# Weight loads and accumulating transfers put on their queues by the planner's due times, in a hybrid attention and recurrence block

## The chip, the cores and the metric

The kernel runs on one core of one Trainium2 chip. The metric is the time of one execution on the device, in microseconds (us); lower is better. The core has a matrix engine (TensorE, PE in the profile, with its weight loads as a row of their own, PEld), VectorE (DVE), ScalarE (ACT), GpSimd (POOL) and SyncE (SP). Each engine works through its own instructions in the order in which the program was written out. Transfers (DMAs) are issued by SP, POOL and ACT; an instruction that issues one waits on its engine's queue until what it needs is there, and what stands behind it on that engine waits with it.

## The reference, cut to what matters

One layer of a residual block on 512 tokens (and 16 learned meta tokens ahead of them) of width 2048. All of it is float32.

```python
h = rms_norm(x, norm_g)
proj = h @ w_in                       # 2048 x 12368
(q_a, k_a, v_a, z_a, q_i, k_i, w_i, q_b, f_b, i_b, z_b, gates) = split(proj)
# branch A: an indexer scores keys, the top 128 are kept per query, attention over them
# branch B: gated linear recurrence in chunks of 64
y = stack([attention * silu(z_a), rms_norm(recurrence) * silu(z_b)])
p = einsum('btnc,ncd->btnd', y, w_branch)      # 2 x 1024 x 2048
merged = sum(sigmoid(gates) * p, axis=2)
return x + merged @ w_out                      # 2048 x 2048
```

## The kernel before, in words

**Products.** A float32 product is made of three TensorE products of rounded parts: every operand is split into a high part (a ScalarE copy that rounds, `wh`) and the remainder (a VectorE subtraction, `wl`). This is done for every weight tile on the way: `hi_lo` (line 417). The three tags of `wh` and of `wl` are used in turn (`NWS = 3`), so the preparation of one operand has to wait for the product that used the tag three operands ago.

**Pairs.** Most of `w_in`, and all of `w_out`, is worked through in *pairs*: a 2x2 block of weights, for which a seven-product scheme (Strassen's, in Winograd's form) takes the place of eight products. There are 44 pairs of `w_in` and 8 of `w_out`. A pair loads four weight chunks of 512 KB, named "11", "21", "22", "12" in this order (line 378), and makes four sums from them:

- the first sum, `s1 = 21 + 22`, and the second, `s2 = s1 + 11`, are VectorE additions into tiles of their own (`sum` in the profile);
- the third, `s3`, is "21" with "11" added in place by an accumulating transfer that POOL issues (`E.dma_add`, line 122, in the profile L123 POOL `raw<-raw`);
- the fourth, `s4`, is "12" with `s2` added in place in the same way (`raw<-sum`).

The seven products run in the order 11, s2, 12, s3, s1, 22, s4 (line 382). Each is 24 matmuls (8 tiles of rows, three parts each), in `run_pair` (line 1549) and, for `w_out`, `run_out` (line 1650). The operand of product i+3 is prepared (`prep_op`, line 487) right after the matmuls of product i are written out, so "12" of a pair is prepared at the end of the pair before.

**What sets the order.** The program is written out by Python code that keeps a clock for each compute engine (`Core`, line 51): every instruction is charged a cost, and starts after what it reads and overwrites. `E.clk["pe"]` is TensorE's clock on this plan, `E.ac[tile]` the time of a tile's last access, `E.wr[tile]` that of its last write. The plan charges an accumulating transfer 4.0 us on POOL and does not cover loads. After every three matmuls `pump` (line 254) lets generator tasks go on (norms, rotary embedding, the recurrence, attention) whose times have come. These tasks write instructions of all engines: on SP the stores and loads that turn k, v and q by way of device memory (`fan`, four DMAs of 64 KB each, line 824; `qay<-qd`, line 874), on POOL other fans, the powers `x ** -0.5` of the norms (line 118) and the gate loads.

**Where the transfers stand.** Before the change a step's transfers are written out right at that step:

```python
def load_upto(i):
    while state["dma"] <= min(i, len(stream) - 1):
        load_chunk(stream[state["dma"]])
        state["dma"] += 1
...
        used = {"s3": 2, "22": 3, "s4": 4}.get(nm)
        if used:
            load_upto(first + used - 1 + NRAW)
```

There are six buffers for weight chunks (`NRAW = 6`). When `s3` has been prepared, the two chunks that go into the buffers of "11" and "21" are queued on SP, when "22" has, the one that goes into its buffer, and when `s4` has, the one into "12"'s. Each waits on SP until the VectorE subtraction, or the accumulating transfer, that uses the buffer last is done. In the seven products, after product 1 the fourth sum of this pair is queued on POOL, and after products 3, 4 and 5 the first, second and third sum of the next pair are made (lines 1587 to 1590, 1705 to 1708).

**Stages.** The nine first jobs are not pairs; their ten low parts (`wl<-raw`) come from accumulating transfers too, which the change does not touch. In the span of the profile the first jobs run until about 145 us, pairs of `w_in` until about 1090 us (k, v and q between 370 and 540 us, then the recurrence), the product with `w_branch` until about 1310 us, and the pairs of `w_out` until the end.

Of the kernel before, what the change touches and what calls it, by code (L numbers as in the profile page):

```python
# [210 lines left out]
def hybrid_kernel(ctx, tc, x, meta, vecs, w_in, rows, w_branch, w_out,  # L211
# [8 lines left out]
    E = Core(nc)  # L220
# [25 lines left out]
    def spawn(gen, prio=1):  # L246
# [4 lines left out]
        tasks.insert(i, t)  # L251
        return t

    def pump(limit=3000.0):
        moved = True
        while moved:
            moved = False
            for t in list(tasks):
                now = E.clk["pe"]
                if t.prio > 5 and hold:  # L260
                    continue
                lim = limit if t.prio < 5 else 1200.0
                if t.t + MARGIN <= now and E.clk["dve"] < now + lim and E.clk["act"] < now + limit:
                    if not t.done and t.step():
                        moved = True
                        break
# [85 lines left out]
    stream = []  # L352
# [31 lines left out]
                preps_.append(op)  # L384
                self.ops.append(op)

    state = {"dma": 0, "split": 0}
    early = []
    NRAW = 6
    NWS = 3  # L390

    def load_chunk(ch):
        j, i = ch["job"], ch["i"]
        r = wp.tile([128, 1024], F32, name=f"raw{i}", tag=f"raw{i % NRAW}")
        nk, k0, c0, nc_ = ch["nk"], ch["k0"], ch["c0"], ch["ncols"]
        src = {"br": w_branch[0, j.n], "out": w_out[0]}.get(j.kind, w_in2)
        v = r[:, :nk * nc_].rearrange("p (k n) -> p k n", k=nk)
        s = src[128 * k0:128 * (k0 + nk), c0:c0 + nc_].rearrange("(k p) n -> p k n", p=128)
        nc.sync.dma_start(v, s)
        ch["raw"] = r  # L400

    def load_upto(i):
        while state["dma"] <= min(i, len(stream) - 1):
            load_chunk(stream[state["dma"]])
            state["dma"] += 1

# [38 lines left out]
    def split_chunk(k, ch):  # L445
        load_upto(ch["i"])
        m = ch["nk"] * ch["ncols"]
        r, nk, n = ch["raw"], ch["nk"], ch["ncols"]
        ch["h"], ch["l"] = [], []
        if k < 4:  # L450
            for g in range(2):
                h, l = slot("eh", F32R), slot("el", F32R)
                w = 4 * n
                E.act(h[:, :w], r[:, w * g:w * g + w], AF.Copy)
                (E.ptt if k > 1 else E.tt)(l[:, :w], r[:, w * g:w * g + w], h[:, :w].bitcast(F32), OP.subtract)
                early.extend((h, l))
                ch["h"] += [h[:, n * i:n * i + n] for i in range(4)]
                ch["l"] += [l[:, n * i:n * i + n] for i in range(4)]
        else:
            j = ch["job"]  # L460
            o = lead(YHOME[j.n], DIST - DBR) if j.kind == "br" else lead((HA, HB)[ch["k0"] // 8], 32)
            h, l = hi_lo(k, r[:, :m], m, o, 0, (n, 24) if j.kind == "br" and j.n == 0 and j.c0 in (0, 1024) else None)
            ch["h"], ch["l"] = cut([h], n), cut(l, n)
        load_upto(ch["i"] + NRAW)

    def sum_1(pr):
        if not hasattr(pr, "s1"):
# [4 lines left out]
    def sum_2(pr):  # L472
        if not hasattr(pr, "s2"):
            pr.s2 = wp.tile([128, 1024], F32, name=f"sum2_{pr.raw['11']['i']}", tag="s2")
            E.tt(pr.s2, pr.s1, pr.raw["11"]["raw"], OP.add)

    def sum_3(pr):
        if not hasattr(pr, "s3"):
            pr.s3 = pr.raw["21"]["raw"]
            E.dma_add(pr.s3, pr.raw["11"]["raw"])  # L480

    def sum_4(pr):
        if not hasattr(pr, "s4"):
            pr.s4 = pr.raw["12"]["raw"]
            E.dma_add(pr.s4, pr.s2)

    def prep_op(k, op):

        pr, nm = op["pair"], op["name"]
        first = pr.raw["11"]["i"]  # L490
        load_upto(first + (0 if nm == "11" else 2 if nm == "s2" else 3))
        raw = {c: ch["raw"] for c, ch in pr.raw.items() if "raw" in ch}
        if nm in raw:
            src = raw[nm]
        else:
            for f in (sum_1, sum_2, sum_3, sum_4)[:int(nm[1]) if nm != "s1" else 1]:
                f(pr)
            src = {"s1": pr.s1, "s2": pr.s2, "s3": raw["21"], "s4": raw["12"]}[nm]
        home, half = HOME[nm]
        if pr.kind == "out":  # L500
            h, l = hi_lo(k, src, 1024, lead(0, MRES[MOP[nm]], True))
        else:
            h, l = hi_lo(k, src, 1024, lead(home, 1056 * half + 4 * (264 - pr.w)), 0 * (nm == "22"))
        w = pr.ncols
        op["h"], op["l"] = cut([h], w), cut(l, w)
        used = {"s3": 2, "22": 3, "s4": 4}.get(nm)
        if used:
            load_upto(first + used - 1 + NRAW)


    cvec = cp.tile([128, 35], F32, name="cvec")
# [1037 lines left out]
    def run_pair(pr, nxt, late, last):  # L1549

        w = pr.w
        bk, W, V = {}, slice(0, w), slice(w, 2 * w)
        for i, (wn, tn, bn, on_) in enumerate(SEVEN):
            op = pr.ops[i]
            split_upto(op["prep"] + 2)
            if not on_:
                bk[bn] = B1.get("p" + bn)
            b = bk[bn][:, W]
            for k in range(8):
                if pr is pairs[0] and i == 1 and k not in placed:  # L1560
                    place_t3(k)
                if pr is pairs[0] and i == 3:
                    place_t4(k)
                th, tl = (t[:, 264 - w:264] for t in (TB[k][tn] if i else (hH[k], hL[k])))
                st_ = k == 0 and not on_
                E.mm(b, op["h"][k], th, st_, False, loose=True)
                E.mm(b, op["h"][k], tl, False, False, loose=True)
                E.mm(b, op["l"][k], th, False, k == 7, loose=True)
                pump(1500.0 if i in (0, 1, 4) and k > 2 else 3000.0)
            if i == 0:  # L1570
                p1 = main_slot("p1")
            elif i == 1:
                E.tt(p1[:, V], p1[:, W], b, OP.subtract)
            elif i == 3:
                E.tt(p1[:, W], b, p1[:, W], OP.subtract)
                B1.put(bk["y"])
            elif i == 4:
                g2 = main_slot("g2")
                E.tt(g2[:, V], p1[:, W], b, OP.subtract)
            elif i == 5:  # L1580
                E.tt(g2[:, W], p1[:, W], b, OP.add)
                B1.put(bk["w"])
            elif i == 6:
                E.tt(g1[:, V], p1[:, V], b, OP.add)
                B1.put(bk["z"])
                S.put(p1)
            if i == 1:
                sum_4(pr)
            if i > 2 and i < 6 and nxt:
                (sum_1, sum_2, sum_3)[i - 3](nxt)  # L1590
            split_upto(op["prep"] + 3)
            if i == 0:
                E.act(p1[:, W], b, AF.Copy)
            if late:
                late.pop(0)()
            if i == 2:
                g1 = main_slot("g1")
                E.act(g1[:, W], b, pr.f)
                B1.put(bk["x"])
            elif i == 5:  # L1600
                late.append(lambda g=g2: pr.done[1](g))
            elif i == 6:
                late.append(lambda g=g1: pr.done[0](g))
            if pr is pairs[-2] and i == 2:
                fetch(0, 0)
            if last:
                if i == 2:
                    fetch(0, 1)
                    first_y.extend(load_y(4, 6, nc.gpsimd))
                elif i == 3:  # L1610
                    S.put(*hH[:8], *hL[:8])
                    for h in range(8):
                        yH[1, h], yL[1, h] = slots("yH", 2, F32R, YHOME[1])
                    while len(y_out) < 8:
                        pump(1e9)
                        if len(y_out) < 8:
                            E.clk["pe"] += 200
                    ysplit = split_y(first_y + [kept[6], kept[7]], 1)
                elif i == 4:
                    S.order = [2, 3, 0, 1]  # L1620
                    S.put(*[t for k in range(8) for t in TB[k]["tiles"][:2]])
                elif i == 5:
                    S.put(*[TB[k]["tiles"][2] for k in range(8)])
                elif i == 6:
                    S.put(*hH[8:], *hL[8:])
                    late.pop(0)()
                    load_gates(1, 0)
                if i in (4, 5):
                    for _ in range(4):
                        next(ysplit, None)  # L1630
# [19 lines left out]
    def run_out(pr, nxt):  # L1650
# [10 lines left out]
        for i, (wn, tn, _, _) in enumerate(SEVEN):  # L1661
# [19 lines left out]
            if r == 1 and not ends:  # L1681
# [20 lines left out]
                else:  # L1702
                    E.tt(q(0, 1), q(0, 1), b, OP.add)
                    store_q(c, 0, 1)
            if i == 1:
                sum_4(pr)
            elif i > 2 and i < 6 and nxt:
                (sum_1, sum_2, sum_3)[i - 3](nxt)
# [390 lines left out]
```

## Time and profile before

| | us |
|---|---|
| median of 3 runs | 1471.97 (1471.61 to 1472.19) |
| the profiled execution | 1472.37 |
| its span in the trace | 1470.6 |
| PE busy / PEld busy | 1446.4 / 1413.1 |
| DVE / ACT / POOL busy | 1188.7 / 715.5 / 270.7 |
| weight loads on SP: 192 of `w_in`, 32 of `w_branch`, 32 of `w_out` | 4.6, 4.9, 4.4 from issue to landing (median) |
| accumulating transfers `raw<-raw` / `raw<-sum`, 52 each | 5.4 / 5.8 from issue to landing (median) |

Matmuls are pipelined, so the busy time of PE holds whatever it is given without a break; only the breaks are idle time. A line of the waits reads: who waited (engine, tile, line) for whom, the sum in us, how often, and the longest. A line of the timeline reads: start, duration, engine, line, operation, tiles as out<-in, shapes, how many in a row, and in brackets the idle time of the engine before it with what ended it. "POOL" and "SPq" lines of a transfer show how long it took to issue, not to land. Tile names carry no numbers: `raw` is any of the six weight chunks.

### The profile page before, as it was taken

To read this page: it belongs to the slowest core of one execution; us is meant where nothing else is said; L and a number is where in the kernel's file an instruction comes from. 1 tells how busy PE (TensorE), PEld (TensorE's weight loads), DVE (VectorE), ACT (ScalarE), POOL (GpSimd) and SP (SyncE) were. 2 spreads that over 40 slices of the span, in tenths; PEclk is the share of its full clock that TensorE was granted. 3 is DMA by queue.
4 is the path that set the end of the run, shared out by engine and by line. 5 is a ranking of instruction groups with operands and counts; after the bars stand their busy time and mean duration, and the time that the engine had idled before them with its cause. 6 is when DMAs were issued, how large, how long until landed. Compare 5 with 4: busy or idle time off the path is not lost.

```text
span 1470.6 us, 33183 instructions
## 1 busy us (share of the span) xinstructions
PE 1446.4 (98%) x13384; PEld 1413.1 (96%) x13384; DVE 1188.7 (81%) x2017; ACT 715.5 (49%) x1172; POOL 270.7 (18%) x344
## 2 busy tenths in 40 slices
PE   7999999999999999999999999999999999999999
PEld 6888999999999999999999999999999999999998
DVE  6789899999988788878787887779676666877776
ACT  5567554544544454444444444444466762434433
POOL 2210000002223320001001010000347410102222
PEclk9999999999999999999999999999999999999999
DMA  9375577788787987678677777858896444558783
GB/s 270 78 166 128 133 175 191 185 200 194 202 207 202 235 205 178 165 173 189 168 192 175 171 182 180 187 135 203 192 279 184 131 121 118 158 137 218 209 222 98
DMA packets 335929, 262.35 MB, mean 178 GB/s; under 512 B 32596, under 2 KB 303520, under 8 KB 335776
## 3 DMA queue, kind: packets, MB, share of 16 engines
q1 hardware_dynamic: 306304, 174.54, 41.6%
q0 software_dynamic: 23968, 79.40, 27.7%
q10 hardware_dynamic: 5504, 6.29, 1.3%
q8 instruction: 105, 1.72, 0.5%
q14 instruction: 48, 0.39, 0.1%
HBM read 170.43 MB, written 29.98 MB: 136 GB/s over the span
## 4 chain that ended last, share of the span: by engine, by line
PE 88%; DMA 4%; DVE 4%; ACT 2%; issue 1%; POOL 1%; SPq 0%; ACTq 0%; DVEq 0%; POOLq 0%
PE px L97 16%; PE pz L97 14%; PE py L97 14%; PE pg L97 12%; PE po L97 9%; PE pw L97 8%; PE pg L99 6%; DMA raw<-sum 2%; PE psc L99 1%; DMA raw<-in_w_in_dram 1%; DVE wl L114 1%; PE phl L99 1%; PE pov L97 1%; ACT wh L107 1%; PE plg L99 1%
## 5 line engine op out<-in xcount | busy, mean ns | idle before, releaser
L107 ACT ACTIVATE wh<-raw 128x1024 fp32r<-128x1024 f32 x306 | 324.1, 1061 | 466.5 <-PE pz L97 110.3
L114 DVE TENSOR_TENSOR wl<-raw,wh 128x1024 fp32r<-128x1024 f32 (+1 forms) x296 | 362.3, 1226 | 107.4 <-ACT wh L107 104.9
L97 PE MATMUL px<-hH,wh 128*128 128x256 f32 (+1 forms) x704 | 200.3, 285 | 3.3 <-ACT p L107 2.9
L97 PE MATMUL px<-hH,wl 128*128 128x256 f32 (+1 forms) x704 | 197.5, 281 | 0.0
L97 PE MATMUL px<-hL,wh 128*128 128x256 f32 (+1 forms) x704 | 197.3, 280 | 0.0
L107 ACT ACTIVATE wh<-sum 128x1024 fp32r<-128x1024 f32 x104 | 110.4, 1062 | 150.3 <-PE pw L97 54.9
L97 PE MATMUL pg<-yH,wh 128*128 128x256 f32 x1024 | 161.7, 280 | 0.6 <-DVE yH L114 0.6
L97 PE MATMUL po<-wh,mh 128*128 128x256 f32 x896 | 154.3, 277 | 0.0
L114 DVE TENSOR_TENSOR wl<-sum,wh 128x1024 fp32r<-128x1024 f32 x104 | 132.6, 1275 | 25.8 <-ACT wh L107 25.6
L97 PEld LDWEIGHTS px<-hH,wh 128*128 128x128 f32 x704 | 133.4, 190 | 4.5 <-ACT p L107 3.3
L97 PEld LDWEIGHTS pg<-yH,wh 128*128 128x128 f32 x1024 | 136.7, 188 | 1.1 <-DVE yH L114 0.8
L97 PEld LDWEIGHTS po<-wh,mh 128*128 128x128 f32 x896 | 135.6, 188 | 0.0
L97 PEld LDWEIGHTS px<-hL,wh 128*128 128x128 f32 x704 | 133.4, 189 | 0.0
L97 PEld LDWEIGHTS px<-hH,wl 128*128 128x128 f32 x704 | 133.2, 189 | 0.0
L97 PE MATMUL pw<-tT,wh 128*128 128x256 f32 (+1 forms) x704 | 129.8, 285 | 1.7 <-DVE attn L1251 1.5
L97 PE MATMUL pz<-tT,wh 128*128 128x256 f32 (+1 forms) x704 | 126.1, 280 | 0.0
L97 PE MATMUL py<-tT,wh 128*128 128x256 f32 (+1 forms) x704 | 125.9, 280 | 0.1
L97 PE MATMUL po<-wl,mh 128*128 128x256 f32 x448 | 124.4, 278 | 1.3 <-DVE wl L114 1.3
L97 PEld LDWEIGHTS pw<-tT,wh 128*128 128x128 f32 x704 | 107.9, 189 | 2.8 <-PE pz L97 2.0
L123 POOL DMA_DIRECT2D raw<-raw x52 | 45.3, 870 | 343.8 <-DVE sum L114 303.3
L97 PEld LDWEIGHTS py<-tT,wh 128*128 128x128 f32 x704 | 107.2, 188 | 0.3 <-issue 0.3
L97 PEld LDWEIGHTS pz<-tT,wh 128*128 128x128 f32 x704 | 107.0, 188 | 0.2
(316 smaller groups left out, 3767.7 us busy)
## 6 DMA issues: line engine op xcount, KB each, us to landing
raw<-in_w_in_dram SPq DMA_DIRECT2D x192, 512.0 KB, 4.6
raw<-raw POOLq DMA_DIRECT2D x52, 512.0 KB, 5.4
raw<-sum POOLq DMA_DIRECT2D x52, 512.0 KB, 5.8
raw<-in_w_branch_dram SPq DMA_DIRECT2D x32, 512.0 KB, 4.9
raw<-in_w_out_dram SPq DMA_DIRECT2D x32, 512.0 KB, 4.4
gd<-g SPq DMA_DIRECT2D x32, 256.0 KB, 5.5
g<-gd POOLq DMA_DIRECT2D x30, 256.0 KB, 3.2
wl<-raw POOLq DMA_DIRECT2D x10, 512.0 KB, 4.6
```

The lines of the kernel that those rows point to most:

```text
L97: self.nc.tensor.matmul(out, lhsT, rhs, start=start, stop=stop, skip_group_check=True)
L99: self.nc.tensor.matmul(out, lhsT, rhs, start=start, stop=stop)
L107: self.nc.scalar.activation(out, in_, f, **kw)
L114: self.nc.vector.tensor_tensor(out, a, b, op=op)
L123: self.nc.gpsimd.dma_start(out, a, accum_op=OP.add)
```

## The change

Three things are changed.

1. **Loads.** Where `prep_op` and `split_chunk` queued the next chunks at once, `load_soon` notes how far loads may go, and `load_due` queues a chunk only if the last access to the buffer's old tile is at most 0.8 us ahead of TensorE's clock on the plan. `pump` calls it after every three matmuls. `load_upto` stays in front of every use as a backstop.
2. **Accumulating transfers.** The third and fourth sum are put on a list with the time at which the plan has their operands ready (the last access to the tile that is added to, or the last write of the other one). `pump` writes them out when TensorE's clock has reached it, ahead of the tasks; the preparation of `s3` or `s4` writes them out if that has not happened.
3. **Place of the fourth sum.** It is put on this list after product 0 of its pair, no longer queued after product 1.

```diff
+    queued = []
+
     def pump(limit=3000.0):
+        load_due()
+        while queued and queued[0][0] <= E.clk["pe"]:
+            queued.pop(0)[1]()
         moved = True
...
-    state = {"dma": 0, "split": 0}
+    state = {"dma": 0, "split": 0, "due": 0}
+    raws = {}
...
         ch["raw"] = r
+        raws[i] = r.tensor.name
...
+    def load_soon(i):
+        state["due"] = max(state["due"], i)
+        load_due()
+
+    def load_due():
+        while state["dma"] <= min(state["due"], len(stream) - 1):
+            old = raws.get(state["dma"] - NRAW)
+            if old and E.ac.get(old, (1e12, 0))[0] > E.clk["pe"] + 800.0:
+                break
             load_chunk(stream[state["dma"]])
             state["dma"] += 1
...
-        load_upto(ch["i"] + NRAW)
+        load_soon(ch["i"] + NRAW)
...
+    def add_soon(pr, key, a, b):
+        def add():
+            if key not in vars(pr):
+                setattr(pr, key, E.dma_add(a, b))
+        t = max(E.ac[a.tensor.name][0], E.wr.get(b.tensor.name, (0.0, 0))[0])
+        queued.append((t, add))
+        queued.sort(key=lambda a: a[0])
+        setattr(pr, "do_" + key, add)
+
     def sum_3(pr):
         if not hasattr(pr, "s3"):
             pr.s3 = pr.raw["21"]["raw"]
-            E.dma_add(pr.s3, pr.raw["11"]["raw"])
+            add_soon(pr, "a3", pr.s3, pr.raw["11"]["raw"])
 
     def sum_4(pr):
         if not hasattr(pr, "s4"):
             pr.s4 = pr.raw["12"]["raw"]
-            E.dma_add(pr.s4, pr.s2)
+            add_soon(pr, "a4", pr.s4, pr.s2)
...
                 f(pr)
+            if nm in ("s3", "s4"):
+                getattr(pr, "do_a" + nm[1])()
...
         if used:
-            load_upto(first + used - 1 + NRAW)
+            load_soon(first + used - 1 + NRAW)
...
-            if i == 1:
+            if i == 0:
                 sum_4(pr)
```

The last edit stands twice, in `run_pair` and in `run_out`.

More of the change, by code (lines that the diff above doesn't have):

```diff
@@ L400, in load_chunk @@
         ch["raw"] = r
+        raws[i] = r.tensor.name
     def load_upto(i):
         while state["dma"] <= min(i, len(stream) - 1):
+            load_chunk(stream[state["dma"]])
+            state["dma"] += 1
+    def load_soon(i):
[6 more added lines that the diff above has]
+                break
             load_chunk(stream[state["dma"]])
@@ L1704, in run_out @@
                     store_q(c, 0, 1)
-            if i == 1:
+            if i == 0:
                 sum_4(pr)
```

## The prediction

> **What bounds the kernel now.** I read the page first. TensorE is busy for nearly the whole span, and no edit takes a matmul away, so the question is how much of its idle time can go.
>
> ```profile
> span 1470.6 us, 33183 instructions
> ...
> PE 1446.4 (98%) x13384; PEld 1413.1 (96%) x13384; DVE 1188.7 (81%) x2017; ACT 715.5 (49%) x1172; POOL 270.7 (18%) x344
> ```
>
> Idle are 1470.6 - 1446.4 = 24.2 us. The waits of TensorE say where the larger pieces are (us in total, times, longest):
>
> ```profile
> PE pc L103 <- DMA vrow<-in_vecs_dram: 7.8, 1, 7.8
> PE px L97 <- ACT p L107: 2.9, 2, 2.0
> PE pz L97 <- DVE g L114: 2.6, 3, 1.3
> PE po L97 <- DVE wl L114: 1.3, 2, 0.9
> PE pz L97 <- ACT km L107: 0.8, 1, 0.8
> ```
>
> The first, 7.8 us, is the start, which the change does not reach. So 24.2 - 7.8 = 16.4 us is more than can be won. The third and fifth lines, four waits, all stand ahead of `pz`, the bank of a pair's last product, which multiplies the fourth sum: 2.6 + 0.8 = 3.4 us. By stage (length, PE, PEld, DVE, ACT, POOL busy, clock, DMA share, GB/s) the k, v and q stage loses 175.0 - 169.8 = 5.2 us, with the granted clock at 0.99, so it is waiting and not a slow clock:
>
> ```profile
> 365.00:540.00 175.00, 169.79 (x1420) 168.18 (x1419) 153.38 (x270) 84.02 (x185) 48.34 (x65) 0.99 0.84 209
> ```
>
> **The fourth sum: what holds it up.** For each of the four waits I looked for when the fourth sum could have started (its "12" is free once VectorE has made `wl` of it) and when POOL issued it. The first, in the timeline of VectorE, POOL and ScalarE, and as the chain of waits has the transfer:
>
> ```profile
> 410.26 1.22 DVE L114 TENSOR_TENSOR wl<-raw,wh 128x1024 fp32r<-128x1024 f32 x1
> 412.39 2.21 POOL L827 DMA_DIRECT2D qd<-qat  x4 [7.79 <-DVE qat L817]
> 414.58 0.96 POOL L123 DMA_DIRECT2D raw<-sum  x1
> 414.58 8.92 DMA raw<-sum
> 423.60 2.01 ACT L107 ACTIVATE wh<-raw 128x1024 fp32r<-128x1024 f32 x2 [4.69 <-DMA raw<-sum]
> ```
>
> "12" was free at 410.26 + 1.22 = 411.48, but POOL's next instruction was a fan that waited for VectorE; the fourth sum left at 414.58, 3.1 us late, landed 8.92 us after that, and ScalarE stood idle for 4.69 us until it could prepare the last operand. The other three are alike (subtraction, fourth sum, and for the last two POOL's instruction in front):
>
> ```profile
> 492.31 1.22 DVE L114 TENSOR_TENSOR wl<-raw,wh 128x1024 fp32r<-128x1024 f32 x1 [0.60 <-ACT wh L107]
> 503.06 0.97 POOL L123 DMA_DIRECT2D raw<-sum  x1
> ...
> 516.37 1.23 DVE L114 TENSOR_TENSOR wl<-raw,wh 128x1024 fp32r<-128x1024 f32 x1
> 522.16 1.01 POOL L118 TENSOR_TENSOR kmy<-kmy,mhalf 16x4 f32<-16x4 f32 x1 [5.08 <-DVE kmy L130]
> 523.13 0.64 POOL L123 DMA_DIRECT2D raw<-sum  x1
> 530.44 1.23 DVE L114 TENSOR_TENSOR wl<-raw,wh 128x1024 fp32r<-128x1024 f32 x1 [2.03 <-ACT wh L107]
> ...
> 716.32 1.22 DVE L114 TENSOR_TENSOR wl<-raw,wh 128x1024 fp32r<-128x1024 f32 x1 [0.59 <-ACT wh L107]
> 724.16 1.03 POOL L118 TENSOR_TENSOR hsq<-hsq,mhalf 128x4 f32<-128x4 f32 x1 [15.53 <-DVE hsq L130]
> 725.16 0.87 POOL L123 DMA_DIRECT2D raw<-sum  x1
> ```
>
> They left 503.06 - 493.53 = 9.5 us, 523.13 - 517.60 = 5.5 us and 725.16 - 717.54 = 7.6 us after "12" was free. In the last two a power stands in front that waits for VectorE's part of a norm.
>
> **The change, part by part.**
>
> *Fourth sum a product earlier.* It is now listed after product 0, with the planned end of that subtraction as its time, and written out in the first calls of `pump` in product 1, ahead of the tasks. A fan or power that tasks write out in product 1 then stands behind it on POOL, no longer in front. In the program the subtraction of "12" comes ahead of the transposition (`qat`), the reduction (`kmy`, `hsq`) or the norm work that those POOL instructions wait for, so the plan's time for the fourth sum is the earlier one. TensorE lost at most 1.3 us at each place, and the fourth sum moves by 3.1 to 9.5 us: all four waits go, **-3.4 us**. What is late next there is VectorE: it stood idle for 2.03 us before its subtraction at 530.44, for want of the `wh`, so it has room. Elsewhere the move gives nothing:
>
> ```profile
> POOL raw L123 <- DVE wl L114: 270.5, 36, 13.2
> raw<-raw POOLq DMA_DIRECT2D x52, 512.0 KB, 5.4
> raw<-sum POOLq DMA_DIRECT2D x52, 512.0 KB, 5.8
> ```
>
> 36 of the 52 fourth sums found POOL already waiting for the subtraction. Behind each fourth sum a power or fan now waits until the subtraction ends and then for 0.64 to 0.97 us of issue (rows above); TensorE's list of waits names POOL nowhere, so I put 0, and at most 0.97 us for one that comes to stand on the path. In the pairs of `w_out` a POOL addition into `xq` is written out at the end of product 0, still ahead of the fourth sum; the 1.3 us of `po` stay.
>
> *Third sum by the list.* It is written out three matmuls later than before, with nothing else of POOL's between. In the first case above it was issued at 403.69 and its reader started at 411.75, on a release by TensorE:
>
> ```profile
> 403.69 0.92 POOL L123 DMA_DIRECT2D raw<-raw  x1 [0.90 <-DVE sum L114]
> 411.75 1.06 ACT L107 ACTIVATE wh<-raw 128x1024 fp32r<-128x1024 f32 x1 [1.80 <-PE px L97]
> ```
>
> 8.06 us less 5.4 us to landing leave 2.7 us; three matmuls are a fraction of that. **0.**
>
> *Loads by due time.* No load leaves before its buffer is free, then or now. What goes is the waiting on SP, and what it holds up:
>
> ```profile
> SPq L399 <- DVE wl L114: 510.7, 128, 13.0
> ```
>
> That is 510.7 / 128 = 4.0 us at each of 128 loads, in which SP's other transfers can't be issued. It shows in the longest wait of the second kind (`px <- ACT p`, 2.0 us). VectorE, SP and ScalarE:
>
> ```profile
> 473.50 0.70 DVE L817 STREAM_TRANSPOSE qT<-qay 128x512 f32<-128x512 f32 x1
> 472.12 5.86 SPq L399 DMA_DIRECT2D raw<-in_w_in_dram  x2
> 478.03 3.50 SPq L827 DMA_DIRECT2D qd<-qT  x4
> 484.66 0.39 SPq L399 DMA_DIRECT2D raw<-in_w_in_dram  x1
> 488.90 4.37 SPq L827 DMA_DIRECT2D vd<-vT  x4
> 493.50 0.34 SPq L874 DMA_DIRECT2D qay<-qd  x1
> 496.16 0.31 ACT L107 ACTIVATE qas<-qay 128x128 f32<-128x128 f32 x1 [3.88 <-DMA qay<-qd]
> ```
>
> The fan of `qT` could go at 474.20 and went at 478.03, behind a load that waited for its buffer: 3.8 us. SP was busy from there to 493.50, when the load of `qay` left that ScalarE then waited 3.88 us for, with the weight preparation behind it. With 3.8 us back ScalarE waits 0.1 us, and TensorE's 2.0 us go: **-2.0 us**. The bounds are 0 (SP's fans take as long, and the wait is filled by them) and 2.0; I take 2.0, since the blocked time is as long as the wait. The other wait of that line, 0.9 us, I leave.
>
> *Loads behind fans.* The same edit lets fans get ahead of a load. The tight load is that of the next pair's "22", which the first sum needs. In one pair:
>
> ```profile
> 371.87 3.56 SPq L399 DMA_DIRECT2D raw<-in_w_in_dram  x2
> 381.62 1.21 DVE L114 TENSOR_TENSOR sum<-raw,raw 128x1024 f32<-128x1024 f32 x1
> 484.66 8.29 DMA raw<-in_w_in_dram
> ...
> raw<-in_w_in_dram SPq DMA_DIRECT2D x192, 512.0 KB, 4.6
> ```
>
> From issue to use 381.62 - 371.87 = 9.75 us. The slowest landing that the chain of waits shows took 8.29 us: 1.46 us to spare. A fan of 4.37 us ahead would make the addition 4.37 - 1.46 = 2.9 us late. It can come ahead only where the plan holds the load back: the buffer's last user is the third sum, which the plan charges 4.0 us after everything else that it charged POOL. So 0 to 2.9 us for an event; for all of the stage I take half of one, **+1.5 us**, nearer to 0 because the median load lands in 4.6 us, and then 9.75 - 4.6 = 5.2 us to spare cover a fan.
>
> *First jobs.* Their loads are queued later too. SP:
>
> ```profile
> 49.59 81.14 SPq L399 DMA_DIRECT2D raw<-in_w_in_dram  x14
> ```
>
> 14 loads in 81.14 us, 5.8 us each, into six buffers: a load is some five chunks, 29 us, ahead of its use. **0**; without that cover, one landing.
>
> [...]
>
> The sum, against the profiled execution's 1472.37 us: -3.4 - 2.0 + 1.5 = -3.9, 1468.5 us. The median of the runs is 0.4 us lower, so **1468.1 us**.
>
> **The rivals.**
>
> *Slower: first sums wait for loads behind fans.* As priced, 2.9 us an event, in the k, v and q stage, where VectorE is busy 153.4 of 175.0 us and can't catch up. Against the gain of 5.4 us it turns the result from the second event on (5.8 us); three make 1472.0 - 5.4 + 8.7 = 1475.3 us. For it: the DMA share is 0.84 there, and fans and loads share SP. Against it: the load keeps its place unless the plan holds it back, and the plan's charge of 4.0 us is below the 5.4 us that the third sum takes to land.
>
> *No change: another wait takes the place.* With VectorE at 88% of the stage, the `g` and `p` steps may come late whatever the transfers do, and every changed due time shifts the tasks that follow. If half of 5.4 us comes back, and the 1.5 us are paid: 1472.0 - 2.7 + 1.5 = 1470.8 us. For it: waits on VectorE's and ScalarE's work make up most of TensorE's list. Against it: in the cases shown VectorE and ScalarE stood idle.
>
> *Fourth sums alone.* The `qay` load stays late since SP is full of fans: 1472.0 - 3.4 + 1.5 = 1470.1 us.
>
> *The list does not act.* If the plan's time were late, the fourth sum would be written out only before `s4` is prepared, two products later than before. Then 5.8 us to landing would lie open in every pair. The time is that of one subtraction already written out, so I give this nothing of its own.
>
> **How the numbers follow.** A measurement of this kernel can tell about 0.2%, 2.9 us, from no change: faster is below 1469.0, slower above 1474.9. Forecast 0.48 (1466.6 without the 1.5 us, 1469.5 with a whole event), fourth sums alone 0.15, another wait 0.22, slower 0.12, better than forecast 0.03 (the 0.9 us of the second `p` and others go too). The first and last, with a few hundredths of the fourth sums alone where nothing is paid (1468.6) and a little of the forecast given back, make 0.52 faster. Same is 0.36, slower 0.12. The range goes from 1465.5 (forecast without cost, and 1.1 us more) to 1474.5, short of three events.
>
> **What would show it.** In the profile after: TensorE's waits for `g` and `km` ahead of `pz` gone or below 1 us in total, and the fourth sum within about 0.5 us of the end of its subtraction at those four pairs; SP's waits at loads for `wl` well below 510.7 us; no ScalarE wait of some 4 us for `qay`; the stage 365 to 540 with some 2 us of lost TensorE time in place of 5.2. Wrong would be VectorE or ScalarE waiting for `raw<-in_w_in_dram`, which today's TensorE waits don't show, or new waits of TensorE of the same sum at other places.

## The result, and the profile after

The changed kernel takes 1465.01 us (1464.01 to 1465.78, 5 runs), the kernel before beside it 1472.19 (1471.61 to 1473.55): ratio 0.995, 95% interval 0.9936 to 0.9965. That is faster, by 7.2 us where 3.9 were forecast, and 0.5 us below the low end of the range. The profiled execution took 1465.78 us, 6.59 less than that of before. The page of after, span and busy times:

```profile
span 1464.0 us, 33193 instructions
...
PE 1444.0 (99%) x13384; PEld 1411.5 (96%) x13384; DVE 1188.7 (81%) x2017; ACT 715.9 (49%) x1172; POOL 271.0 (19%) x344
```

TensorE idles for 1464.0 - 1444.0 = 20.0 us, 4.2 less than before. Its busy time fell too, by 2.4 us, with the same 13384 matmuls. The prediction looked only for idle time; fewer busy microseconds for the same matmuls point to the clock, and the windows below bear that out. The waits of TensorE after (in all, times, longest):

```profile
PE pc L103 <- DMA vrow<-in_vecs_dram: 7.8, 1, 7.8
...
PE po L97 <- DVE wl L114: 1.4, 2, 0.9
PE pz L97 <- DVE g L114: 1.3, 2, 1.0
...
PE px L97 <- DVE g L114: 0.9, 1, 0.9
PE px L97 <- ACT p L107: 0.7, 1, 0.7
PE pw L97 <- DVE p L114: 0.5, 1, 0.5
```

Of the 3.4 us ahead of `pz` 1.3 are left, and 0.9 and 0.5 us are new. The wait of 2.0 us for `p` is gone. The k, v and q stage after:

```profile
365.00:540.00 175.00, 172.34 (x1460) 171.30 (x1459) 157.97 (x276) 86.88 (x188) 49.47 (x66) 1.00 0.88 217
```

It loses 2.7 us in place of 5.2. The clock is 1.00 where it had been 0.99, and this small digit is the main finding. The windows of the kernel before around its longest wait (length, PE, PEld, DVE, ACT, POOL busy, clock, DMA share, GB/s):

```profile
494.00:496.00 2.00, 2.00 (x20) 2.00 (x20) 1.59 (x6) 0.00 (x0) 0.00 (x0) 1.00 0.73 200
496.00:498.00 2.00, 0.73 (x7) 0.52 (x5) 0.00 (x0) 1.84 (x9) 0.00 (x0) 1.00 1.12 337
498.00:500.00 2.00, 1.29 (x6) 1.30 (x7) 1.58 (x3) 1.60 (x3) 0.14 (x1) 0.67 0.55 168
500.00:502.00 2.00, 2.00 (x11) 2.00 (x11) 2.00 (x4) 0.00 (x0) 2.00 (x4) 0.50 0.53 122
502.00:504.00 2.00, 2.00 (x19) 2.00 (x18) 1.82 (x6) 0.76 (x1) 2.00 (x5) 0.97 1.07 320
```

TensorE is idle from 496.73 to 498.70. Then its clock is halved, by the clock records from 498.70 for 3.413 us: 11 matmuls in 2 us where 20 fit before. The same stretch of after has no idle time and full clock:

```profile
496.00:504.00 8.00, 8.00 (x71) 8.00 (x71) 7.78 (x14) 3.73 (x10) 6.23 (x10) 1.00 1.05 265
```

The load of `qay` that ended this wait stood behind the fan of `kT` on SP before, and stands ahead of it after (one line of before, two of after; before, the load left at 493.50, as the prediction shows):

```profile
485.09 3.76 SPq L827 DMA_DIRECT2D kd<-kT  x4
...
484.71 0.34 SPq L904 DMA_DIRECT2D qay<-qd  x1
...
485.60 4.47 SPq L857 DMA_DIRECT2D kd<-kT  x4
```

Following the same matmul through both traces shows where the 6.6 us come from (place in the trace of before; us gained, the start-up and the end of the kernel left out):

| place | gained |
| --- | --- |
| 496.73: the wait itself, and the half clock behind it | 2.13 + 1.72 |
| 734.74, fourth sum | 1.0 |
| 1093.06, first product of `w_branch` | 0.8 |
| 511.65 to 540, fourth sums and a new wait of 0.86 | 0.6 |
| 470.77, a wait of 0.41 | 0.7 |
| 990.58, a wait of 0.94 before, 0.66 after | 0.3 |
| 426.65, fourth sum: 1.26 before; 0.47 and 1.03 after | -0.2 |

Each kernel has one profiled execution, so the small rows need care: at 990.58 the wait is 0.61 us in the run below that moves only the load of `qay`, and under 0.25 us in the one that moves one more transfer, though neither moves anything near that place.

### The profile page after: what moved, and what is told of

It is laid out like the page before. It is cut to its first block, busy times and chain, and to the rows that moved or that the text cites. A ratio compares the mean times of both kernels' runs of the same rounds, so it can differ in the third digit from the quotient of the medians.

```text
span 1464.0 us, 33193 instructions
## 1 busy us (share of the span) xinstructions
PE 1444.0 (99%) x13384; PEld 1411.5 (96%) x13384; DVE 1188.7 (81%) x2017; ACT 715.9 (49%) x1172; POOL 271.0 (19%) x344
## 3 DMA queue, kind: packets, MB, share of 16 engines
q8 instruction: 105, 1.72, 0.5%
## 4 chain that ended last, share of the span: by engine, by line
PE 89%; DVE 4%; DMA 3%; issue 2%; ACT 1%; POOL 1%; SPq 0%; ACTq 0%; DVEq 0%; POOLq 0%
PE px L97 16%; PE pz L97 15%; PE py L97 14%; PE pg L97 12%; PE po L97 9%; PE pw L97 8%; PE pg L99 6%; PE psc L99 1%; DVE wl L114 1%; PE phl L99 1%; PE pov L97 1%; PE plg L99 1%; PE pho L99 1%; ACT wh L107 1%; PE ppt L103 1%
```

## The experiments

A half of the change each, then single waits, then the clock, then loads held back longer. Medians of one row stand beside the kernel before on the same chip.

| run | median (lowest to highest) | before beside it | ratio, interval |
| --- | --- | --- | --- |
| loads alone | 1467.13 (1466.04 to 1467.86) | 1473.94 | 0.9948, 0.9935 to 0.9961 |
| transfers alone | 1469.64 (1468.51 to 1472.18) | 1473.94 | 0.9971, 0.9960 to 0.9982 |
| before, `qay` on POOL | 1473.79 (1472.28 to 1475.72) | 1473.94 | 0.9994, 0.9984 to 1.0004 |
| before, `qay` on POOL and one fourth sum early | 1467.41 (1466.57 to 1469.24) | 1473.67 | 0.9962, 0.9950 to 0.9974 |
| changed, masks on POOL | 1463.69 (1462.97 to 1465.60) | 1473.67 | 0.9937, 0.9921 to 0.9953 |
| changed, no list | 1474.91 (1472.31 to 1488.49) | 1473.67 | 1.0012, 0.9989 to 1.0034 |
| transfers alone, masks on POOL | 1465.07 (1464.41 to 1465.66) | 1472.80 | 0.9946, 0.9929 to 0.9962 |
| changed, loads 4 us late | 1462.39 (1462.07 to 1463.64) | 1472.80 | 0.9928, 0.9913 to 0.9943 |
| changed, loads 8 us late | 1470.53 (1467.73 to 1475.45) | 1473.38 | 0.9981, 0.9971 to 0.9990 |
| changed, loads 4 us late, masks on POOL | 1462.47 (1462.28 to 1462.93) | 1473.38 | 0.9925, 0.9910 to 0.9940 |

**Loads alone.** The changed kernel with the transfers put back as they were (the main lines, against the changed kernel):

```diff
-        while queued and queued[0][0] <= E.clk["pe"]:
-            queued.pop(0)[1]()
...
-            add_soon(pr, "a4", pr.s4, pr.s2)
+            E.dma_add(pr.s4, pr.s2)
...
-            if i == 0:
+            if i == 1:
                 sum_4(pr)
```

> The kernel before with the loads queued by due time alone; both accumulating transfers as before (fourth sum behind the second product). No engine but SP has its order changed. Theory 1, the freed load queue takes away TensorE's 1.97 us wait for `qay` at 496.73 and the stretch behind it in which TensorE ran at half clock (3.41 us, about 1.9 us lost): 3.9 us of the 7.2 are gained here, 1468.3. Theory 2, the wait went because the fourth sum's new place changed the plan, which now writes the load of `qay` ahead of the fan of `kT` on SP: here that order is the old one, the wait stays, and the time is 1472 within 1 us.

Measured: 1467.13 us; the profiled execution is 5.2 us shorter than that of before, with no half clock until the end of the kernel (mean granted clock 1.000). Theory 1 holds for this half; 0.6 us at 426.65 and 0.8 us at 1093.06 come on top. The fans on SP keep their old order, `kT` ahead of `qay`, but they run earlier, since the load that waited for its buffer now stands behind the fan of `qT`. SP here:

```profile
473.55 1.79 SPq L842 DMA_DIRECT2D qd<-qT  x4
...
481.28 3.06 SPq L842 DMA_DIRECT2D kd<-kT  x4
484.44 3.58 SPq L842 DMA_DIRECT2D vd<-vT  x4
488.25 0.53 SPq L889 DMA_DIRECT2D qay<-qd  x1
```

The fan that went at 478.03 goes at 473.55, and the load of `qay` at 488.25, not 493.50. What is late next is the fourth sum of the same pair: TensorE waits 1.36 us ahead of `pz` at 507.20, where it had waited 0.60.

**Transfers alone.** The list and the place of the fourth sum, with `load_upto` where the changed kernel has `load_soon`.

> The kernel before with the list of accumulating transfers and the fourth sum behind the first product; loads as before, each written as soon as its predecessor's last reader is. Theory 1: only the shorter waits ahead of the last product are gained, some 2 to 3 us, 1469 to 1470, and the `qay` wait with its half clock is still there. Theory 2: SP has the load of `qay` ahead of the fan of `kT` here too; the wait and the half clock go, 1465 to 1466.5.

Measured: 1469.64 us, on theory 1's side in size, but the reason is a third. The `qay` wait is 0.91 us here, not 1.97, as the load of `qay` does stand ahead of the fan of `kT`; so each half of the change shortens or removes this wait, the half clock behind it goes with both, and their gains overlap (5.2 and 3.3 us by the profiled executions, 6.6 together). In exchange a wait of 2.13 us came up at 423.05, with half clock behind it (0.63 in the window from 426 to 428 us, 0.51 in that from 428 to 430). VectorE there:

```profile
415.97 1.22 DVE L114 TENSOR_TENSOR wl<-sum,wh 128x1024 fp32r<-128x1024 f32 x1
421.95 0.20 DVE L348 CAST masks<-mf 128x64 uint8<-128x64 f32 x1 [4.76 <-DMA mf<-in_masks_dram]
```

**The wait alone.** Kernel before, one instruction moved.

```diff
-        nc.sync.dma_start(y[:, :512], d)
+        (nc.gpsimd if d is qd_[4] else nc.sync).dma_start(y[:, :512], d)
```

> The kernel before with one instruction moved: the load of `qay` that left SP at 493.50 is issued by POOL, right behind the fourth sum that POOL issued at 476.75. All else in its old order. If the wait cost its idle time alone: 1.97 us gained, 1470.2. If it also set off the half clock behind it: 1.97 + 1.9 = 3.9 us, 1468.3, and the profile shows no stretch at half clock before the end.

Measured: no gain, 1473.79 us beside 1473.94, though the wait at 496.73 is gone. Following the matmuls, 2.13 + 1.72 us are won at just that place, as with the whole change; 3.1 us are lost again within 15 us (the rest later). The half clock is not gone but moved:

```profile
508.00:510.00 2.00, 0.14 (x1) 0.17 (x2) 1.84 (x3) 2.00 (x9) 0.00 (x0) 1.00 1.13 257
510.00:512.00 2.00, 2.00 (x16) 2.00 (x17) 2.00 (x3) 1.27 (x3) 0.00 (x0) 0.83 0.98 216
512.00:514.00 2.00, 2.00 (x11) 2.00 (x11) 1.53 (x3) 0.10 (x2) 0.33 (x1) 0.50 0.97 245
```

TensorE is idle for 2.16 us from 507.70. POOL issues the fourth sum behind a fan, and ScalarE waits for it (timelines of both):

```profile
498.27 2.26 POOL L827 DMA_DIRECT2D qd<-qat  x4
500.49 0.97 POOL L123 DMA_DIRECT2D raw<-sum  x1
...
507.06 2.00 ACT L107 ACTIVATE wh<-raw 128x1024 fp32r<-128x1024 f32 x2 [6.52 <-DMA raw<-sum]
```

**The wait and one fourth sum.** To the run just told, one more edit, in one pair (two lines of it; at the old place the plan is still charged for the transfer, so that nothing else moves):

```diff
+            if i == 0 and pr is pairs[17]:
+                nc.gpsimd.dma_start(pr.raw["12"]["raw"], pr.s2, accum_op=OP.add)
```

> The kernel with the `qay` load on POOL, and in the same pair alone the fourth sum written a product earlier, ahead of the power for `qay` on POOL; the plan's clocks as before, so nothing else moves. If the wait of 2.16 us that came up at 507.70 there (with half clock behind it) is the late fourth sum, it goes, the 3.85 us won at the `qay` wait stay, and the run is at 1468 to 1469 with no half clock. If it is something else (VectorE's or ScalarE's own work), the wait stays and the time is 1472 to 1474.

Measured: 1467.41 us, no half clock before the end (mean granted clock 1.000). POOL now, with the transfer ahead of the power:

```profile
493.95 0.89 POOL L1591 DMA_DIRECT2D raw<-sum  x1 [1.77 <-DVE wl L114]
497.73 1.03 POOL L118 TENSOR_TENSOR qay<-qay,mhalf 128x4 f32<-128x4 f32 x1 [2.89 <-DVE qay L130]
```

4.7 us are won at this place, and 0.8 lost again at 528.37, where the fourth sum of the next pair now keeps TensorE waiting for 1.56 us. So 3.9 us stay of two moved transfers, about as much as the whole change wins at 496.73; neither needs the due times. By the profiled executions the run is 5.0 us shorter than before (1472.37 to 1467.35), but 0.5 of them are the start-up and 1.0 stand at 990.58, where nothing was moved.

**The masks.** The changed kernel with `nc.gpsimd` for `nc.sync` at the load `mf<-in_masks_dram`.

> The changed kernel with the load of the masks, on which VectorE stood idle for 3.10 us at 417.69 to 420.79, issued by POOL ahead of the fourth sum in place of SP at 413.35. If that idle is what kept the earlier fourth sum from paying in this pair, the two gaps of TensorE behind it (0.47 and 1.03 us) shrink to under 0.5 us together: 1 to 1.4 us less than the changed kernel, 1463.6 to 1464. If VectorE is late there for its own work (maxima and weight parts queued), they stay and the time is 1465.

Measured: 1463.69 us. VectorE in the changed kernel, and behind it in this run:

```profile
420.79 0.20 DVE L349 CAST masks<-mf 128x64 uint8<-128x64 f32 x1 [3.10 <-DMA mf<-in_masks_dram]
```

```profile
417.50 0.18 DVE L349 CAST masks<-mf 128x64 uint8<-128x64 f32 x1
```

Both gaps of TensorE behind it are gone, 1.9 us by the same matmuls. So at 426.65 the fourth sum did come earlier in the changed kernel (issued 0.3 us after its subtraction, not 3.1), but another wait stood ready to take its place.

**Transfers alone, masks on POOL.** The same edit on the old loads.

> The kernel with the list and the early fourth sum but the old loads, and the load of the masks on POOL as in the run on the changed kernel. There TensorE waited 2.13 us at 423.05 with half clock behind it, while VectorE stood idle for 4.76 us for the masks. If the masks are the cause, that gap and the half clock go: 2.1 + 1.6 us less than 1469.6, about 1466. If not, the time stays near 1469.6. Beside the changed kernel with the masks on POOL (1463.7) it also says what the loads by due time add once neither wait is there: by the first theory some 2 us.

Measured: 1465.07 us, the gap at 423.05 and its half clock gone (mean granted clock 1.000). Beside the changed kernel with the masks on POOL the loads by due time add less than the 2 us expected: 1.4 us by the medians, which come from two chips, and 1.2 us by the same matmuls with the start-up left out. The `qay` wait is still 1.28 us here, at 493.41, with no half clock behind it; with loads by due time it is gone, and a wait of 0.71 us at 507.99 takes part of that back.

**No list.** The changed kernel, transfers written where they are asked for, the fourth sum behind the first product.

```diff
-        queued.append((t, add))
-        queued.sort(key=lambda a: a[0])
+        add()
```

> The changed kernel without the list: both accumulating transfers are written where they are asked for, the fourth sum right behind the first product; loads by due time. If the place behind the first product is what pays, 1465 to 1466 as the changed kernel. If the list matters (it lets what POOL has ready go ahead of a transfer whose operands aren't ready), POOL stands at the fourth sum with fans behind it, and the time is 1467 or more, no better than the loads alone.

Measured: 1474.91 us: all is lost. In the first pair the fourth sum is now asked for before the third and stands ahead of it on POOL. It can't go until VectorE, busy with other work, has made the low part of "12" (146.08 to 147.31; the bracket names the scores, which VectorE does next). POOL, and ScalarE that waits for the third sum (landed at 154.55):

```profile
147.60 0.85 POOL L123 DMA_DIRECT2D raw<-sum  x1 [21.38 <-DVE score L135]
148.14 1.18 POOL L123 DMA_DIRECT2D raw<-raw  x1
...
154.62 1.06 ACT L107 ACTIVATE wh<-raw 128x1024 fp32r<-128x1024 f32 x1 [7.05 <-issue]
```

TensorE is idle for 4.76 us from 151.24, at half clock behind that (0.50 in the window from 156 to 158 us), and again after 2.24 us at 542.52. In the changed kernel the third sum of that pair leaves at 135.12. Here an early place without an order by operands is worse than the late one (loads alone, 1467.13 us).

**The clock.** Two runs delay the third product of every other pair in the changed kernel, by writing its `wh` several times with the same values:

```diff
+        n = STALL.get(k, 0)
+        while n > 0:
+            nc.scalar.activation(h[:, :min(n, m)], src[:, :min(n, m)], AF.Copy)
+            n -= m
         E.act(h, src, AF.Copy)
```

> The changed kernel with nine deliberate delays in the recurrence: ScalarE writes the `wh` of the third product of nine pairs several times over (4 to 10 extra copies of 1 us), with 2 pairs between two of them, so that TensorE stands idle for lengths that differ. If the half clock follows any idle of about 2 us or more, each gap from there up is followed by 3.41 us at half clock, and none below. [...] If the two had nothing to do with one another, half clock comes at places that don't answer to the gaps. Each gap costs its length, and about 1.9 us more where half clock follows.

> The changed kernel with ten delays like those of the stalls run, now 4.25 to 5.75 extra copies of `wh`, for idle times of some 1.4 to 3 us. In the runs so far all starts of a half clock stand at whole multiples of 3.413 us from one another, and within the window of 3.413 us that ends at such a start TensorE was idle for 1.95 us or more; idle of 1.69 us within one window started none. If the rule is that share of one window on a fixed raster, gaps with over 1.95 us in one window are followed by half clock, those split by a window's end with under 1.69 us on either side are not, though they may be as long. If it is the length of the gap alone, the line falls between two lengths whatever the raster.

Measured: 1522.25 and 1508.28 us in one execution each. A gap of 2.26 us was followed by no half clock, one of 1.82 us was, and one of 3.26 us was not. The last two, in windows of the second run, the one of 3.26 us first:

```profile
779.00:782.00 3.00, 1.66 (x15) 1.46 (x13) 0.79 (x1) 2.94 (x4) 0.00 (x0) 1.00 0.01 3
782.00:785.00 3.00, 1.09 (x10) 1.12 (x11) 3.00 (x7) 1.51 (x4) 0.85 (x1) 1.00 0.71 190
785.00:788.00 3.00, 3.00 (x27) 2.92 (x26) 2.18 (x4) 1.57 (x4) 0.00 (x0) 1.00 1.10 264
...
537.00:540.00 3.00, 1.50 (x12) 1.50 (x13) 2.89 (x4) 2.92 (x5) 0.85 (x1) 1.00 0.12 23
540.00:543.00 3.00, 3.00 (x16) 3.00 (x16) 2.34 (x4) 0.24 (x1) 0.00 (x0) 0.50 1.03 195
```

In these two the length alone does not decide. The starts of half clock within a run stand at whole multiples of 3.413 us from one another (in the kernel before at 498.70 and, at its end, at 1471.50: 972.80 us, 285 times 3.4133). So a row of windows of that length, the raster, was laid over each trace through these starts. TensorE's idle time (by the ends of matmuls as the trace models them) was added up in each window of that raster, from 20 us to the last matmul of all fourteen traces (before, after and twelve runs). In these traces it separates the cases cleanly:

```text
window of 3.413 us at full clock    idle in it       half clock next
the gap of 3.26 us, split in two    1.54 and 1.72    no, no
largest four without                1.69 1.72 1.80 1.81   no
smallest four with                  1.82 1.95 1.96 2.06   yes (1.96: the kernel before)
all windows with 1.82 or more       19               yes, every one
```

So in these traces half clock came behind every window at full clock with 1.82 us or more of idle time, 53% of it, and behind none with 1.81 us or less.

By the rows above, the half clock behind the wait of 1.97 us in the kernel before is, by estimate, partly chance. A gap of that length has 1.82 us in one window at about half of the places at which the raster can stand (an estimate from 1.97, 1.82 and 3.413 us). How many of the other executions of that kernel had it is not on record.

**Loads held back longer.**

```diff
-            if old and E.ac.get(old, (1e12, 0))[0] > E.clk["pe"] + 800.0:
+            if old and E.ac.get(old, (1e12, 0))[0] > E.clk["pe"] - 4000.0:
```

> The changed kernel with every weight load held back further: queued only when the plan has its buffer free for 4 us, in place of 0.8 us before that. If the blocked queue was the cost and a load has the cover that the prediction took from its rows (1.5 to 5.2 us), SP's waits for `wl` fall from 457 us to under 200 and the time is within 2 us of 1465. If loads behind fans are the danger (the slower rival), VectorE and ScalarE wait for `raw<-in_w_in_dram`, TensorE behind them, and the time is 1475 or more.

Measured: 1462.39 us, less than the changed kernel's 1465.01, which was not measured beside it, and 3.5 us less by the profiled executions; 2.0 us of these stand at the masks, which left SP at 409.99 here and at 413.35 in the changed kernel. SP's waits in the changed kernel, then here:

```profile
SPq L405 <- DVE wl L114: 456.9, 120, 13.0
```

```profile
SPq L405 <- DVE wl L114: 360.9, 83, 13.0
```

They fall by a fifth, not by more than half as expected: 83 loads still find their buffer busy; why was not tried. With -8000.0:

> The changed kernel with loads queued only when the plan has had their buffer free for 8 us. At 4 us the time was 1462.4 and VectorE waited 2.2 us in all for loads. If the slower rival has a point from which it decides, it lies here: 4 us more than there is beyond the slack of 1.5 us that the worst landing leaves, and the first sums wait some 2 to 4 us in many pairs: 1470 or more. If the loads still have cover, 1461 to 1463.

Measured: 1470.53 us; the profiled execution, at 1475.45, was the longest of the ten. VectorE's waits for the weights, at 4 us and at 8 us:

```profile
DVE sum L114 <- DMA raw<-in_w_in_dram: 2.2, 3, 0.9
```

```profile
DVE sum L114 <- DMA raw<-in_w_in_dram: 19.2, 14, 3.6
```

Here is the slower rival's mechanism, first sums that wait for their loads, but it needs loads held back by some 9 us more than the change does. With the masks on POOL as well, at 4 us:

> The changed kernel with loads held back until the buffer has been free for 4 us and the masks loaded by POOL. If the later loads gained by letting the masks' load go earlier (1.9 of their 3.5 us stand at that pair), the two don't add up: 1462 to 1463. If they gained elsewhere, 1460.5.

Measured: 1462.47 us: the two don't add up. The two versions with loads held for 4 us, at 1462.4 us, are the shortest of all runs; the changed kernel was not measured beside them, and their ratios to the kernel before (0.9928 and 0.9925, beside its 0.995) have intervals that overlap with its own. Between the start and the end no stretch is at half clock in them (mean granted clock 1.000 in both).

## Why the prediction was wrong

The direction was right, and the places it named are those where most of the time went. The gain was undersized, and its split over the terms was wrong.

- **Step that failed: loads by due time, "-2.0 us", with 2.0 as the upper bound.** The chain named (SP blocked, `qay` late, ScalarE waits 3.88 us, TensorE 2.0) is right: the load went at 484.71 and ScalarE no longer waited. But the wait cost 1.97 us of idle time and 1.9 at half clock and behind it, 3.85 together, and the bound of 2.0 had no room for the second part. The text met the trace of it and dismissed it: "the granted clock at 0.99, so it is waiting and not a slow clock". One hundredth of 175 us is 1.75 us, as much as the term it stood beside. That the half clock stood behind this wait in the profiled execution is in part chance, as told above, so 3.85 is the price in this execution and not in every one.
- **Fourth sum, "all four waits go, -3.4".** At 511.65 and 734.74 the wait is gone, at 532.93 it is 0.30; at 426.65 it was replaced by a wait for VectorE, itself waiting for the masks. Some 1.4 us came in all, with a new wait of 0.86 us at 510.20 counted in. "In the cases shown VectorE and ScalarE stood idle" was true, but VectorE's idle time for the masks (quoted below) stood in the list of waits of before and wasn't used. The transfer was within 0.5 us of its subtraction at two of the four places only; at the others it left 4.2 and 1.9 us after, still behind a power, which the prediction had ruled out. The first of them after the change (lines of VectorE and POOL):

```profile
491.92 1.23 DVE L114 TENSOR_TENSOR wl<-raw,wh 128x1024 fp32r<-128x1024 f32 x1 [0.60 <-ACT wh L107]
495.43 1.92 POOL L118 TENSOR_TENSOR qay<-qay,mhalf 128x4 f32<-128x4 f32 x1 [3.75 <-DVE qay L130]
497.31 0.88 POOL L123 DMA_DIRECT2D raw<-sum  x1
```

- **Loads behind fans, "+1.5".** No such cost showed: held back by 4.8 us more, the loads made the kernel no slower (1462.39 us). The wait of 0.86 us that is new at 510.20 in the changed kernel isn't there with the loads alone; in the changed kernel VectorE does the norm of `kay` ahead of the addition (`g<-p,pw`, at 510.50) that TensorE then waits for.
- **SP's waits "well below 510.7"**: 456.9. What counted was not the sum but the one load that stood ahead of a fan.
- **Third sum by the list, "0"**: right against the kernel before, but the list is what keeps the early fourth sum from standing ahead of the third; without it the change is no faster than before.
- **"Fourth sums alone"** was given 1470.1 as a rival; run as an experiment it was 1469.6, by another route: the `qay` wait halved, the one for the masks grown.
- **"Better than forecast"** was given 0.03, for waits like the second one for `p`. That wait went from 0.94 to 0.66 us only; the half clock is what took the time below the range.

The wait of VectorE that the second point means, from the waits of the kernel before:

```profile
DVE masks L344 <- DMA mf<-in_masks_dram: 2.7, 1, 2.7
```

By the profiled executions 3.9 us were forecast and 6.6 came: 1.9 for the half clock and 1.5 not paid on one side, some 2 missing from the fourth sums on the other, and 1.5 at two places not named (470.77 and 1093.06). So errors of both signs cancelled in part, and that the number came as near as it did is partly luck. The 0.8 us at 1093.06 come with the loads alone too; why was not tried.

## What to carry to other kernels

Price a wait of TensorE by what the clock does behind it: read the granted clock in windows of a few microseconds around every gap near 2 us, since here a mean of 0.99 over 175 us hid 1.9 us, about as much as the wait of 1.97 itself. Ask of each wait that is removed which operand is late next, for in this kernel one removed wait, worth 3.9 us, gave 3.1 back within 15 us, and with the next one removed too 3.9 us stayed. On an in-order queue, put transfers in the order in which their operands are ready; early alone was slower here (1.0012 of the kernel before without the list, 0.995 with it).

## What the runs showed of the hardware that was not expected

- In the fourteen traces the clock of TensorE was halved for at least 3.413 us after every window of 3.413 us of the raster with 1.82 us or more of idle time, and after no window at full clock with 1.81 or less. The raster did not stand at the same place in every execution: half clock started at 498.70 in the kernel before, at 511.32 with `qay` on POOL and at 155.68 without the list (the last two worked out from granted clocks of 0.83 from 510 to 512 us and 0.92 from 154 to 156 us), which leave 0.35, 2.73 and 2.08 us over whole multiples of 3.4133 us. Waits of 2.17 and 2.72 us were followed by half clock, those of 2.48 and 2.75 us were not, all in the second run with delays. Whether this makes the spread of the kernel before (1470.3 to 1478.3 us over all chips) was not tried.
- The load of the masks took 7.4 us to land from SP at 413.35 in the changed kernel, 4.0 us from SP at 412.75 with the loads alone, and 3.5 us from POOL at 410.66. The two from SP differ by 3.4 us; what makes the difference was not tried.
